# Encoder layer on one core: dealing branch B's gate and projection products over the units, with keys ahead of queries in the second half

## The chip, the core and the metric

One core of a Trainium2 chip runs the kernel. Its engines work side by side and each follows its own queue in order: PE (TensorE, matrix products), DVE (VectorE), ACT (ScalarE), POOL (GpSimd) and SP (SyncE, which issues most DMAs). The metric is the device time of one execution in microseconds (us). Three executions took 2141.36, 2141.90 and 2141.91, median 2141.9. A separate execution was recorded by the profiler.

## The reference

A bidirectional encoder layer on a prompt of 1024 tokens and a sample of 512, width 1024, inputs in float32:

```python
z = xn @ w_in                    # q_A k_A v_A q_B k_B v_B gate_A gate_B
o_a = grouped-query attention with axial rotary embedding (8 heads of 64)
o_b = neighbourhood attention on a grid 64 wide: windows of 8 rows x 16 columns,
      plus a learned bias per head and offset (8 heads of 64)
merged = sigmoid(ga) * (o_a @ w_proj_a) + sigmoid(gb) * (o_b @ w_proj_b)
x = x + merged @ w_out
x = x + relu(rmsnorm(x) @ w_mlp_up) ** 2 @ w_mlp_down
y = rmsnorm(x)
```

The change concerns `o_b` of the prompt, the projections `q_B` and `k_B`, and the product of `gate_B`, which runs between them.

## The kernel before

The sample goes through branches A and B and the merge first, then the prompt, then both together through the MLP (from about 1200 us). Operands are kept as a high and a low part in a 32-bit format that PE takes at full rate, and a product is three matmuls (high by high, high by low, low by high): `mm3`, L216. One such triple of 128 x 128 by 128 x 512 is called a *step*. Making the two parts is `split`: ACT copies the high part (L199), DVE subtracts for the low part in two halves (L206).

**Branch B of the prompt** runs in 32 *units* (h, j): head h of 8, and a strip j of the grid in the order 1, 2, 0, 3. I number them: unit u = 4h + place of j, so unit 14 is (3, 0). Its tiles carry h and j: `sbs_3_0` are its scores. In each pass i of the main loop, in this order:

- `s_unit`: PE makes unit i's scores in `sbs` (four matmuls, PSUM pool of two). POOL makes the masks `bms`, DVE adds them (`sbss`, L1039), ACT takes the exponential (`pbs`, L1065), DVE a reciprocal, POOL scales.
- `turn`, one unit later: DVE transposes blocks (L1077), POOL writes them to DRAM (`tbs`, L1079).
- `fetch_t`, two units later: SP reads them back turned (`bhs`, L1088), behind what stands on SP by then; `prep_v` loads the values `vss` of the next head.
- `t_unit`, three units later: ACT and DVE make the high and low part of `bhs` (L1099, L1100).
- `v_unit`, four units later, at the end of that pass: PE makes the outputs `obs` from six matmuls; ACT and DVE add their halves (`ot_Bs`, `os_Bs`), SP stores.
- Between them PE is filled by *gate steps* (`fill.pull(f)`: `gpss`, 8 weight chunks of 16 steps each for the two halves of 512 tokens; a chunk's `raw_gs` is loaded and `w_gs` split while the chunk before is worked on) and by *projection steps* of the next pair of heads (`qkproj`: `pqbs` queries, `pkbs` keys, 8 steps for each half of the tokens). The projection of a pair of heads is done in the seventh and eighth unit of the pair before. Its outputs are taken from PSUM by ACT and DVE: queries L978 and L980, keys L999 and L1001, one DMA (L1005).

The projection's weights are loaded by `load_qk` and split by entries of `held`, one at a time at fixed passes.

PE runs this stretch in the order in which the code stands. The other engines' orders are fixed when the program is built, by a scheduler that places each instruction by when its inputs are due; `note` and `behind` put scores, exponentials and fetches behind certain weight splits (L186 to L195). `fill.drain` at pass 25 empties the gate, and projection A (`ppas`, `w_pas`) follows; its output halves `oXs` are split in between.

Of the kernel before, what the change touches and what calls it, by code (L numbers as in the profile page):

```python
# [20 lines left out]
NC8 = D // P  # L21
# [40 lines left out]
def encoder(ctx: ExitStack, tc: tile.TileContext, xs, outs, w):  # L62
# [30 lines left out]
    def mm(name):  # L93
        return pmm.tile([P, 512], F32, tag="mm", name=name)
# [91 lines left out]
    def note(engine, op):  # L186
        if held_pe:
            firm[engine].append(op.ins)
# [230 lines left out]
    def run(tr, nxt, first):  # L419
        N, x, T, NT, NB = tr.N, tr.x, tr.T, tr.NT, tr.NB  # L420
# [107 lines left out]
        for g in range(2):  # L528
            with phase(f"phR{N}_{g}") as ph:
# [28 lines left out]
                held = [] if first and fresh else None  # L558
# [354 lines left out]
        with phase(f"phB{N}") as ph:  # L913
# [41 lines left out]
            def qkproj(pr, wqk, dest):  # L955
                wq, wk = wqk
                qT = slot([P, 2, T], F32R, f"qB{N}_{pr}")
                kT = [slot([P, 2, T], F32R, f"kB{N}_{pr}_{e}") for e in range(2)]
                dest[pr] = (qT, kT)
                for tb in range(NB):  # L960
                    cs = slice(tb * 512, tb * 512 + 512)
                    pq = mm(f"pqb{N}_{pr}_{tb}")
                    for k in range(NC8):
                        mm3(pq, wq[k][0], wq[k][1], xh(tb, k), xl(tb, k), k == 0, k == NC8 - 1)
                        yield
                    for e in range(2):
                        hs = slice(64 * e, 64 * e + 64)
                        ls = slice(64 - 64 * e, 128 - 64 * e)

                        src = pq[hs].rearrange("p (r j c) -> p j r c", j=4, c=16)  # L970

                        def strip_view(s_):
                            return qT[s_, e, :].rearrange("p (j r c) -> p j r c", j=4, c=16)[
                                :, :, tb * 8 : tb * 8 + 8, :
                            ]

                        dst_h, dst_l = strip_view(hs), strip_view(ls)
                        note("ACT", nc.scalar.activation(dst_h, src, AF.Copy, scale=0.125))  # L978
                        for jj in range(4):
                            op = nc.vector.scalar_tensor_tensor(  # L980
                                dst_l[:, jj],
                                src[:, jj],
                                0.125,
                                dst_h[:, jj].bitcast(F32),
                                op0=ALU.mult,
                                op1=ALU.subtract,
                            )
                            note("DVE", op)
                    pk = mm(f"pkb{N}_{pr}_{tb}")
                    for k in range(NC8):  # L990
                        mm3(pk, wk[k][0], wk[k][1], xh(tb, k), xl(tb, k), k == 0, k == NC8 - 1)
                        yield
                    for e in range(2):
                        hs = slice(64 * e, 64 * e + 64)
                        ls = slice(64 - 64 * e, 128 - 64 * e)

                        both = (hs, ls) if e == 0 else (hs,)
                        for os_ in both:
                            nc.scalar.activation(kT[e][os_, 0, cs], pk[hs], AF.Copy)  # L999
                        for os_ in both:  # L1000
                            nc.vector.tensor_tensor(  # L1001
                                kT[e][os_, 1, cs], pk[hs], kT[e][hs, 0, cs].bitcast(F32), op=ALU.subtract
                            )
                        if e == 1:
                            nc.gpsimd.dma_start(kT[e][ls, :, cs], kT[e][hs, :, cs])  # L1005

            qk = {}
            def s_unit(u, before=None):
                h, j = u
                ct = (0, 1, 1, 2)[j]  # L1010
                c0 = (0, 8, 24, 32)[j]
                jr = (16, 8, 8, 0)[j]
                s = big(f"sb{N}_{h}_{j}")
                for hf in range(halves):
                    r0 = 0 if hf == 0 else 4
                    ir = 4 if hf == 0 else 0
                    if j != 2:
                        bm = ph.tile([P, nkey], F32, tag="bm", name=f"bm{N}_{h}_{j}_{hf}", bufs=4)
                        nc.gpsimd.tensor_tensor(
                            bm.rearrange("p (r c) -> p r c", c=32),  # L1020
                            rects[h][:, ir : ir + kr_n, jr : jr + 32],
                            msk[:, hf * 3 + ct, :].rearrange("p (r c) -> p r c", c=32),
                            op=ALU.add,
                        )
                        bms[hf] = bm
                    q0 = j * (T // 4) + hf * P
                    so = s[:, hf * 512 : hf * 512 + nkey]
                    for i in range(2):
                        kv = qk[h // 2][1][h % 2][:, i, :].rearrange("p (r c) -> p r c", c=GRID_W)[
                            :, r0 : r0 + kr_n, c0 : c0 + 32  # L1030
                        ]
                        mul(so, qk[h // 2][0][:, h % 2, q0 : q0 + P], kv, start=(i == 0), stop=(i == 1))
                sums = []
                for hf in range(halves):
                    nm = f"{N}_{h}_{j}_{hf}"
                    sb = ph.tile([P, nkey], F32, tag="sb", name=f"sbs{nm}", bufs=2)
                    nm_ = sml.tile([P, 1], F32, tag="nm", name=f"nmb{nm}")
                    with behind("DVE"):
                        nc.vector.tensor_tensor_reduce(  # L1039
                            out=sb,  # L1040
                            in0=s[:, hf * 512 : hf * 512 + nkey],
                            in1=bms[hf],
                            op0=ALU.add,
                            op1=ALU.min,
                            scale=-1.0,
                            scalar=3e38,
                            accum_out=nm_,
                        )
                    sums.append((sb, nm_))
                if before is not None:  # L1050
                    before()
                ps = []
                pm = ph.tile([P, halves * nkey], F32, tag="pb", name=f"pb{N}_{h}_{j}", bufs=4 // halves)
                if u in moved:
                    pm = pm.rearrange("p (b f k i) -> p b f k i", b=4, f=halves, i=32)
                for hf, (sb, nm_) in enumerate(sums):
                    nm = f"{N}_{h}_{j}_{hf}"
                    l = sml.tile([P, 1], F32, tag="l", name=f"lb{nm}")
                    p = pm[:, :, hf] if u in moved else pm[:, hf * nkey : (hf + 1) * nkey]
                    to, of = p, sb  # L1060
                    if u in moved:
                        to = p.rearrange("p b k i -> p k b i")
                        of = sb.rearrange("p (k b i) -> p k b i", b=4, i=32)
                    with behind("ACT"):
                        nc.scalar.activation(to, of, AF.Exp, bias=nm_, scale=-1.0, accum_out=l)  # L1065
                    rl = sml.tile([P, 1], F32, tag="rl", name=f"rlb{nm}")
                    nc.vector.reciprocal(rl, l)
                    nc.gpsimd.tensor_scalar(p, p, rl, 1.0, op0=ALU.mult, op1=ALU.mult)
                    ps.append(p)
                PT[u] = pm if u in moved else ps  # L1070
# [103 lines left out]
            for i in range(n + 4 - NB):  # L1174
                if moved:
                    slot_no[0] = i
                if i < n - 8:
                    f = (5 if i < 2 else 2 + i % 2) if NB == 1 else 5 - (i % 6 == 5)
                else:
                    f = 3 + i % 2 if NB == 1 else 8  # L1180
                if NB == 2 and i == n - 11:
                    pa = proj_a(ph, raw_here)
                    next(pa)
                if i < n:
# [10 lines left out]
                    if moved and h > 0:  # L1195
                        with behind("SP"):
                            prep_v(h, j)
                    if i % 8 == 6 and i + 2 < n:

                        qp = qkproj(i // 8 + 1, wqk, qk)  # L1200
                        for _ in range(NC8):
                            next(qp)
                    if i % 8 == 7 and qp is not None:
                        for _ in qp:
# [15 lines left out]
                if NB == 1 and i == n - 8:  # L1220
                    fill.drain()
                    fill.add(pa)
                if held and (i in (4, 5) if i < 8 else i % 8 in (2, 4)):
                    held.pop(0)()
                if i == 3:
                    wqk = load_qk(1, held)
                if oa_held and i >= (n - 9 if NB == 2 else n - 11):
                    oa_held.pop(0)()
                if qp is not None and NB == 2:
                    for _ in range(NC8):  # L1230
                        next(qp)
                fill.pull(f - f // 2)
                for u in due_v.get(i, ()):
# [726 lines left out]
```

## Time and profile before

| | before |
|---|---|
| median of three executions | 2141.9 us |
| profiled execution | 2144.5 us |
| its span (first to last instruction) | 2142.7 us |
| granted clock of TensorE, mean | 0.996 |
| PE busy | 2102.9 us (98%) |
| DVE busy | 1484.2 us (69%) |
| ACT busy | 1141.0 us (53%) |
| POOL busy | 374.0 us (17%) |
| prompt's branch B units on PE | 798.6 to 998.2 us, then projection A |

The profile takes one execution. Its lines give a start, a duration, the engine, the source line and the tile; in square brackets stands the idle time before an instruction and what released it. A granted clock of 0.5 in a stretch means TensorE at half speed there. A wait whose releaser is not known is called "issue".

### The profile page before, as it was taken

The numbers are of one execution on the slowest core, as the hardware profiler recorded it, in microseconds if no ns is written. First come the engines' busy times: TensorE is split into PE (matmuls) and PEld (weight loads), VectorE is DVE, ScalarE is ACT, GpSimd is POOL, SyncE is SP. The second block draws the span as 40 slices with busy tenths as digits, with TensorE's granted clock in tenths as the row PEclk, the third lists the DMA queues.
The fourth block names the chain that finished last, engine by engine and source line by source line (L and its number), as shares of the span: only waits on it lengthen the run. The fifth ranks groups of instructions, "written<-read, shape, count | busy, mean of one in ns | idle before, by whom it ended". The sixth has DMA issues, their size and how long they took to land.

```text
span 2142.7 us, 32014 instructions
## 1 busy us (share of the span) xinstructions
PE 2102.9 (98%) x10871; PEld 1841.3 (86%) x10871; DVE 1484.2 (69%) x2793; ACT 1141.0 (53%) x2487; POOL 374.0 (17%) x470
## 2 busy tenths in 40 slices
PE   9999999999999999989999999999999999999998
PEld 8888778988897888877888899999999988888886
DVE  6665786767657756766882877778777777659662
ACT  6664653767656645544531566566655633334442
POOL 2232310323233215533200200003000000000000
PEclk9999999999999999999999999999999999999999
DMA  6437557520122136666572666578544799688561
GB/s 190 133 97 212 156 159 252 184 73 25 54 80 70 42 95 190 206 206 184 176 247 101 209 193 192 164 252 208 159 145 158 260 353 341 213 274 279 165 206 59
DMA packets 337002, 372.95 MB, mean 174 GB/s; under 512 B 33471, under 2 KB 269639, under 8 KB 336839
## 3 DMA queue, kind: packets, MB, share of 16 engines
q1 hardware_dynamic: 296695, 296.17, 44.6%
q10 hardware_dynamic: 31072, 45.11, 6.0%
q0 software_dynamic: 9072, 29.63, 4.7%
q8 instruction: 86, 1.41, 0.3%
q14 instruction: 77, 0.63, 0.1%
HBM read 274.29 MB, written 97.32 MB: 173 GB/s over the span
## 4 chain that ended last, share of the span: by engine, by line
PE 52%; DVE 1%; issue 0%; DMA 0%; ACT 0%; SPq 0%; POOLq 0%; POOL 0%; ACTq 0%; DVEq 0%
PE dn L212 20%; PE ua L212 6%; PE ud L212 6%; PE uc L212 6%; PE ops L212 4%; PE ub L212 3%; PE ppbs L212 2%; PE ppas L212 2%; PE dnf L212 2%; PE pt L353 0%; PE obs L212 0%; PE gpss L212 0%; PE sbs L212 0%; PE ptbs L1109 0%; DVE A L1435 0%
## 5 line engine op out<-in xcount | busy, mean ns | idle before, releaser
L212 PE MATMUL dn<-wd,ah 128*128 128x512 f32 x1248 | 384.3, 389 | 0.0
L212 PEld LDWEIGHTS dn<-wd,ah 128*128 128x128 f32 x1248 | 234.3, 188 | 48.6
L212 PE MATMUL dn<-wd,al 128*128 128x512 f32 x624 | 242.8, 389 | 0.0
L1434 ACT ACTIVATE ah<-ar 128x512 fp32r<-128x512 f32 x168 | 103.9, 627 | 197.5 <-PE dn L212 186.1
L212 PE MATMUL gpss<-xs_0h,w_gs 128*128 128x512 f32 x512 | 189.7, 404 | 0.8 <-DVE ot_Bs L471 0.4
L1435 DVE TENSOR_TENSOR al<-ar,ah 128x512 fp32r<-128x512 f32 x168 | 113.8, 686 | 74.1 <-ACT ah L1434 66.9
L212 PE MATMUL ud<-B,A 128*128 128x384 f32 x768 | 143.6, 334 | 0.7 <-DVE c L1552 0.7
L212 PE MATMUL uc<-B,A 128*128 128x384 f32 x768 | 143.7, 334 | 0.0
L212 PE MATMUL ua<-B,A 128*128 128x384 f32 x768 | 138.8, 334 | 0.0
L212 PEld LDWEIGHTS dn<-wd,al 128*128 128x128 f32 x624 | 117.2, 188 | 24.2
L780 POOL TENSOR_SCALAR ps<-ps,rls 128x1024 f32<-128x1024 f32 (+1 forms) x96 | 96.9, 1010 | 225.7 <-DVE rls L779 200.4
L212 PEld LDWEIGHTS ud<-B,A 128*128 128x128 f32 x768 | 134.0, 188 | 1.1 <-DVE c L1552 1.1
L212 PEld LDWEIGHTS uc<-B,A 128*128 128x128 f32 x768 | 134.1, 188 | 0.2 <-ACT A L1434 0.2
L212 PEld LDWEIGHTS ua<-B,A 128*128 128x128 f32 x768 | 133.7, 188 | 0.2
L820 DVE TENSOR_TENSOR ptls<-pTs,pths 128x512 fp32r<-128x512 f32 x160 | 107.6, 686 | 37.7 <-ACT pths L819 36.9
L819 ACT ACTIVATE pths<-pTs 128x512 fp32r<-128x512 f32 x160 | 94.1, 598 | 73.9 <-PE pTs L814 71.6
L212 PE MATMUL ops<-wh_os,mgs 128*128 128x512 f32 x384 | 119.5, 390 | 0.0
L774 DVE TENSOR_REDUCE nms<-ss 128x1 f32<-128x1024 f32 (+1 forms) x96 | 99.8, 1040 | 25.6 <-PE ss L772 25.0
L212 PEld LDWEIGHTS gpss<-xs_0h,w_gs 128*128 128x128 f32 x512 | 97.1, 190 | 19.1 <-DVE w_gs L206 0.7
L180 POOL TENSOR_TENSOR rs_f<-ms_f,mhalf 128x1 f32<-128x1 f32 x6 | 4.0, 666 | 590.7 <-DVE ms_f L176 590.7
L777 ACT ACTIVATE ps<-ss,nms 128x1024 f32<-128x1024 f32 (+1 forms) x96 | 93.3, 972 | 22.7 <-DVE nms L774 20.1
L814 PEld LDWEIGHTS pTs<-ident,ps 128*128 128x128 f32 x640 | 77.9, 140 | 28.5 <-POOL ps L780 4.5
(288 smaller groups left out, 5158.5 us busy)
## 6 DMA issues: line engine op xcount, KB each, us to landing
ar<-ud SPq DMA_DIRECT2D x120, 512.0 KB, 5.1
br<-in_w_mlp_down_dram SPq DMA_DIRECT2D x72, 512.0 KB, 5.4
rawu<-in_w_mlp_up_dram SPq DMA_DIRECT2D x64, 512.0 KB, 4.2
ud<-c ACTq DMA_DIRECT2D x128, 192.0 KB, 2.8
raw_gs<-in_w_in_dram SPq DMA_DIRECT2D x32, 512.0 KB, 4.0
ud<-cs SPq DMA_DIRECT2D x64, 192.0 KB
tbs<-pbs POOLq DMA_DIRECT2D x24, 384.0 KB, 3.4
bhs<-tbs SPq DMA_DIRECT2D x96, 96.0 KB, 2.2
```

The lines of the kernel that those rows point to most:

```text
L180: nc.gpsimd.tensor_tensor(r[:, :n], m[:, :n], mhalf[:, :n], op=ALU.pow)
L212: op = nc.tensor.matmul(out, a, b, **kw)
L774: nc.vector.tensor_reduce(nm_, s, axis=AX.X, op=ALU.max, negate=True)
L777: nc.scalar.activation(p, s, AF.Exp, bias=nm_, accum_out=l)
L780: nc.gpsimd.tensor_scalar(p, p, rl, 1.0, op0=ALU.mult, op1=ALU.mult)
L814: nc.tensor.transpose(pt[:, j * P : (j + 1) * P], PP[u, j][:, kc * P : (kc + 1) * P], ident)
L819: nc.scalar.activation(hi, pt, AF.Copy)
L820: nc.vector.tensor_tensor(lo, pt, hi.bitcast(F32), op=ALU.subtract)
L1434: nc.scalar.activation(hi, src, AF.Copy)
L1435: nc.vector.tensor_tensor(lo, src, hi.bitcast(F32), op=ALU.subtract)
```

## The change

It touches branch B of the prompt (`NB == 2`); the sample's keeps its numbers. There are four parts.

1. `qkproj` projects queries of the first half, keys of the first half, **keys of the second half, then queries of the second half** (before: queries, keys, queries, keys).
2. The gate steps per unit are 8, 7, 7, 6, 6, 0, 0, 4 over eight units (before: 5, and 4 in every sixth).
3. The projection starts in the sixth unit of eight: 4 + 4 steps there, 6 + 6 in the seventh, the other 12 in the eighth (before: 8 + 8 in the seventh and 16 in the eighth).
4. `load_qk(1)` and the two splits of its weights come one pass earlier.

```diff
-                for tb in range(NB):
+                def queries(tb):
                     cs = slice(tb * 512, tb * 512 + 512)
                     pq = mm(f"pqb{N}_{pr}_{tb}")
...
+                def keys(tb):
+                    cs = slice(tb * 512, tb * 512 + 512)
                     pk = mm(f"pkb{N}_{pr}_{tb}")
...
+                yield from queries(0)
+                yield from keys(0)
+                if NB == 2:
+                    yield from keys(1)
+                    yield from queries(1)
...
-                if i < n - 8:
-                    f = (5 if i < 2 else 2 + i % 2) if NB == 1 else 5 - (i % 6 == 5)
+                if NB == 1:
+                    f = (5 if i < 2 else 2 + i % 2) if i < n - 8 else 3 + i % 2
                 else:
-                    f = 3 + i % 2 if NB == 1 else 8
+                    f = (8, 7, 7, 6, 6, 0, 0, 4)[i % 8] if i < n - 8 else 8
...
-                    if i % 8 == 6 and i + 2 < n:
+                    if i % 8 == (6 if NB == 1 else 5) and i < n - 2 - 8 * (NB - 1):
 
                         qp = qkproj(i // 8 + 1, wqk, qk)
-                        for _ in range(NC8):
+                    if qp is not None and i % 8 < 7:
+                        for _ in range(NC8 if NB == 1 else 2 * (i % 8) - 6):
                             next(qp)
...
-                if held and (i in (4, 5) if i < 8 else i % 8 in (2, 4)):
+                if held and (i % 8 in (2, 4) if i > 7 else i in ((4, 5), (3, 4))[NB - 1]):
                     held.pop(0)()
-                if i == 3:
+                if i == 4 - NB:
                     wqk = load_qk(1, held)
...
                 if qp is not None and NB == 2:
-                    for _ in range(NC8):
+                    for _ in range(2 * (i % 8) - 6):
                         next(qp)
```

Three places of the built programs show what it does to the engines' orders; the numbers at the end of names tell buffers apart.

On **PE** at the end of unit 13 and the start of unit 14. Before, unit 14's scores were followed by the first query steps:

```order
L212 MATMUL obs_2_2_10443<-bhs_2_2_10272,vss_2_10059 128x2x128 x6
L212 MATMUL sbs_3_0_10457<-kBs_1_1_9773,qBs_1_9771 128x384 x4
L212 MATMUL pqbs_2_0_10498<-xs_0h_4501,w_bqs_2_9986 128x512
L212 MATMUL pqbs_2_0_10498<-xs_0l_4503,w_bqs_2_9986 128x512
L212 MATMUL pqbs_2_0_10498<-xs_0h_4501,w_bqs_2_9986 128x512 x2
```

Now the queries of the first half stand in unit 13, and the keys follow the scores:

```order
L212 MATMUL obs_2_2_10487<-bhs_2_2_10291,vss_2_10056 128x2x128 x6
L212 MATMUL sbs_3_0_10501<-kBs_1_1_9742,qBs_1_9740 128x384 x4
L212 MATMUL pkbs_2_0_10549<-xs_0h_4501,w_bks_2_9989 128x512
L212 MATMUL pkbs_2_0_10549<-xs_0l_4503,w_bks_2_9989 128x512
L212 MATMUL pkbs_2_0_10549<-xs_0h_4501,w_bks_2_9989 128x512 x2
```

The first product behind these scores now needs the keys' weight `w_bks_2`, and no query step stands in front of it.

On **DVE**, where the outputs of unit 13 (`ot_Bs_3_2`) are added up. Before, the low part for unit 14's outputs (`bhs_3_0`, L1100) came after the split of gate weight 6, unit 17's scores (`sbss_4_2`) and a transpose:

```order
L471 TENSOR_TENSOR ot_Bs_3_2_10879<-obs_3_2_10872,ot_Bs_3_2_10879 64x512
L206 TENSOR_TENSOR w_gs_3328_6_10727<-raw_gs_3328_6_0_10725,w_gs_3328_6_10727 128x512 x2
L1039 ISA sbss_4_2_0_10826,nmbs_4_2_0_10827<-sbs_4_2_10821,bms_4_1_0_10747 128x384
L1039 ISA nmbs_4_2_0_10827 128x1
L1039 ISA sbss_4_2_1_10829,nmbs_4_2_1_10830<-sbs_4_2_10821,bms_4_1_1_10751 128x384
L1039 ISA nmbs_4_2_1_10830 128x1
L1077 STREAM_TRANSPOSE pbs_4_1_10764<-pbs_4_1_10764 128x768
L1067 RECIPROCAL rlbs_4_2_0_10838<-lbs_4_2_0_10836 128x1
L1067 RECIPROCAL rlbs_4_2_1_10843<-lbs_4_2_1_10841 128x1
L1100 TENSOR_TENSOR bhs_3_0_10775<-bhs_3_0_10775 128x768
```

Now it stands ahead of them:

```order
L471 TENSOR_TENSOR ot_Bs_3_2_10890<-obs_3_2_10883,ot_Bs_3_2_10890 64x512
L1110 TENSOR_TENSOR bhs_3_0_10763<-bhs_3_0_10763 128x768
L483 TENSOR_TENSOR os_Bs_3_2_10893<-ot_Bs_3_2_10890 64x256
L206 TENSOR_TENSOR w_gs_3328_6_10782<-raw_gs_3328_6_0_10780,w_gs_3328_6_10782 128x512 x2
L1049 ISA sbss_4_2_0_10828,nmbs_4_2_0_10829<-sbs_4_2_10823,bms_4_1_0_10735 128x384
L1049 ISA nmbs_4_2_0_10829 128x1
L1049 ISA sbss_4_2_1_10831,nmbs_4_2_1_10832<-sbs_4_2_10823,bms_4_1_1_10739 128x384
L1049 ISA nmbs_4_2_1_10832 128x1
L1087 STREAM_TRANSPOSE pbs_4_1_10752<-pbs_4_1_10752 128x768
```

`bhs_3_0` moved up past one split, two score rows and a transpose; the split of gate weight 6, which unit 18 now uses from its third gate step on, moved behind it and behind `os_Bs_3_2`.

On **SP**, the load of gate weight 7. Before, it stood behind the fetches of units 16 and 17 (`bhs_4_1`, `bhs_4_2`), and that weight was first used in unit 22:

```order
L1088 DMA bhs_4_1_10914<-tbs_4_1_10833 32x4x192 x4
L942 DMA vss_4_10782<-vds_4660 32x4x128 x4
L1238 DMA zgs_1_4662<-sgs_3328_5_0_10861 128x512
L1238 DMA obds_4664<-os_Bs_3_2_10882 64x256
L1088 DMA bhs_4_2_10986<-tbs_4_2_10901 32x4x192 x4
L942 DMA vss_4_10782<-vds_4660 32x4x128 x4
L245 DMA raw_gs_3328_7_0_11000<-in_w_in_dram 128x8x128
```

Now it follows unit 16's fetch and four loads of values:

```order
L1249 DMA zgs_1_4662<-sgs_3328_4_1_10778 128x512
L1249 DMA obds_4664<-os_Bs_3_1_10820 64x256
L1098 DMA bhs_4_1_10926<-tbs_4_1_10835 32x4x192 x4
L942 DMA vss_4_10770<-vds_4660 32x4x128 x4
L245 DMA raw_gs_3328_7_0_10943<-in_w_in_dram 128x8x128
L1249 DMA zgs_1_4662<-sgs_3328_5_0_10860 128x512
```

The load moved up by one fetch, one load of values and two stores; the weight's first use moved from unit 22 to the last gate step of unit 20, and on DVE its split stands directly ahead of unit 19's score rows.

## The prediction

> **What bounds the kernel now.** I read the page first, then PE's waits in the prompt's branch B (its units run from 798 to 998 us), then the busy shares by stretch, then the stalls one at a time.
>
> ```profile
> span 2142.7 us, 32014 instructions
> PE 2102.9 (98%) x10871; PEld 1841.3 (86%) x10871; DVE 1484.2 (69%) x2793; ACT 1141.0 (53%) x2487; POOL 374.0 (17%) x470
> ```
>
> TensorE (PE) is busy 98% of the span, so only its idle time and a slow clock can be won. The change leaves the number of its products alone. From here everything is PE's lost time in branch B. Its waits between 770 and 1070 us (engine, tile, what ended the wait: total, times, longest):
>
> ```profile
> PE obs L212 <- issue: 6.8, 2, 4.7
> PE sbs L212 <- DVE kBs L1001: 2.3, 2, 1.8
> PE ppas L212 <- DVE w_pas L206: 1.5, 1, 1.5
> ...
> PE pqbs L212 <- DVE ot_Bs L471: 0.7, 1, 0.7
> ...
> PE obs L212 <- DVE bhs L1100: 0.2, 1, 0.2
> ```
>
> The `ppas` wait is behind the units, and this change leaves its surroundings alone. The other rows add up to 6.8 + 2.3 + 0.7 + 0.2 = 10.0 us. The busy shares by stretch (start:end, length, PE busy, then the granted clock after POOL) show where they lie:
>
> ```profile
> 798.00:857.00 59.00, 58.35 (x274) 48.92 (x273) 41.85 (x99) 30.17 (x61) 29.28 (x37) 1.00 0.61 185
> 857.00:918.00 61.00, 60.31 (x295) 51.42 (x294) 43.90 (x108) 32.20 (x65) 30.54 (x38) 1.00 0.69 207
> 918.00:987.60 69.60, 62.77 (x292) 53.09 (x291) 45.80 (x112) 34.61 (x67) 24.39 (x34) 0.95 0.69 203
> ...
> 942.30:949.20 6.90, 5.89 (x18) 5.25 (x19) 3.26 (x6) 1.84 (x4) 0.74 (x2) 0.51 0.80 226
> 990.00:993.60 3.60, 3.60 (x10) 3.00 (x10) 3.51 (x9) 2.58 (x6) 1.11 (x2) 0.53 0.57 174
> ```
>
> The first 16 units lose 1.3 us together. The third round of eight, from 918 us, loses 6.8 us and runs partly at half clock. The two short stretches are those at half speed: from the end of the 4.68 us stall below, 943.31, to 949.2 is 5.9 us, at half speed 2.9 us of work lost; 3.4 us from 990 lose 1.7 us. So the units lose **10.0 + 4.6 = 14.6 us**, and that is all the change can win. The three long stalls:
>
> ```profile
> 933.52 0.72 PE L212 MATMUL obs<-bhs,vss 128*128 128x256 f32 x4 [2.14 <-issue]
> 943.31 1.62 PE L212 MATMUL obs<-bhs,vss 128*128 128x256 f32 x6 [4.68 <-issue]
> 989.81 1.11 PE L212 MATMUL sbs<-kBs,qBs 128*128 128x384 f32 x3 [1.82 <-DVE kBs L1001]
> ```
>
> "issue" names no releaser, so I looked at what makes `bhs` for these two products, on DVE and ACT:
>
> ```profile
> 928.86 1.29 DVE L206 TENSOR_TENSOR w_gs<-raw_gs,w_gs 128x512 fp32r<-128x512 f32 x2 [0.27 <-ACT w_gs L199]
> 930.07 0.55 DVE L1039 CUSTOM_DVE_ANT_0 sbss<-sbs,bms 128x384 f32<-128x384 f32 x1
> ...
> 932.23 1.09 DVE L1100 TENSOR_TENSOR bhs<-bhs 128x768 fp32r<-128x768 f32 x1
> ...
> 942.25 0.96 DVE L1100 TENSOR_TENSOR bhs<-bhs 128x768 fp32r<-128x768 f32 x1 [0.57 <-ACT bhs L1099]
> 940.77 0.61 ACT L1065 ACTIVATE pbs<-sbss,nmbs 128x384 f32<-128x384 f32 x1 [2.85 <-DMA tbs<-pbs]
> 941.39 0.83 ACT L1099 ACTIVATE bhs<-bhs 128x768 fp32r<-128x768 f32 x1
> ```
>
> Unit 14's low part (932.23) is queued on DVE behind the gate weight's split and unit 17's scores; it ends where PE resumes. Unit 15's high part (941.39) stands on ACT behind an exponential of unit 19, which waits 2.85 us for the buffer that unit 17's transposed block leaves. Both are queue positions, not missing data.
>
> **The change part by part.** PE's own times: a gate or projection step is three products.
>
> ```profile
> 870.64 0.39 PE L212 MATMUL gpss<-xs_1h,w_gs 128*128 128x512 f32 x1
> 870.87 0.89 PE L212 MATMUL obs<-bhs,vss 128*128 128x256 f32 x6
> 871.60 0.88 PE L212 MATMUL sbs<-kBs,qBs 128*128 128x384 f32 x4
> 872.31 0.40 PE L212 MATMUL gpss<-xs_1h,w_gs 128*128 128x512 f32 x1
> ```
>
> By the starts, a product takes 0.23 us, so a step 0.69; a unit's `obs` 0.73 and its scores 0.71. Eight units hold 70 steps before (38 gate, 32 projection) and 70 after: no work is removed, only dealt differently.
>
> *What goes.* In the new order unit 14's low part stands on DVE ahead of the gate weight and of unit 17's scores, and unit 15's high part on ACT ahead of the exponentials of units 18 and 19. Their blocks are fetched a unit earlier than they are used. I take 2.14 + 4.68 + the 2.9 of half clock as gone: **-9.7**. The 0.69 (unit 15's projection, which opens an accumulator and waits until `obs` output has left one) goes, since unit 15 now goes on with one already open, and the 0.16 before an early `obs` goes too, since the unit that it ends is longer: **-0.85**. The first unit's 0.49 and unit 24's 1.82 with its 1.7 change their cause and are priced again below. Nothing of the 14.6 is then left but what follows.
>
> *Keys first.* Units 6, 14 and 22 now begin with keys. Their weight's split is queued behind the previous unit's `obs` output:
>
> ```profile
> 885.55 0.87 PE L212 MATMUL sbs<-kBs,qBs 128*128 128x384 f32 x4
> 885.75 0.59 ACT L470 ACTIVATE ot_Bs<-obs 64x512 f32<-64x512 f32 x1 [3.52 <-PE obs L212]
> 886.25 1.04 ACT L199 ACTIVATE w_bks<-raw_bks 128x1024 fp32r<-128x1024 f32 x1
> 887.32 1.29 DVE L206 TENSOR_TENSOR w_bks<-raw_bks,w_bks 128x512 fp32r<-128x512 f32 x2 [0.27 <-ACT w_bks L199]
> ```
>
> `obs` ended as the next scores began, at 885.55. The high part is done 1.74 us later, the first low half 2.4. Before, eight query steps hid that; now the scores alone do, 0.71 us. PE waits 1.0 for the high part and, as the low part is first used by a step's third product, 0.3 more: 1.3 each in units 14 and 22 (unit 6's weight is split in units 3 and 4): **+2.6**. Were the split's inputs early and the queue free, 0; without any overlap 1.7 each.
>
> *Gate weight 6.* It is first used in unit 18's third gate step, 0.71 + 2 x 0.69 = 2.1 us after unit 13's `obs` at the end of unit 17, low half 2.55 after. DVE now does that `obs`'s output (about 1.4 us after it ended), unit 14's low part (0.96), the sum's second half (0.4) and then the first half of the split (0.65): 3.4. **+0.9**, from 0 to 1.3.
>
> *Gate weight 7.* Its load is now directly behind unit 16's fetch on SP, and that waits for unit 16's transposed block:
>
> ```profile
> 930.71 1.79 POOL L1019 TENSOR_TENSOR bms<-rects,msks 128x384 f32<-128x384 f32 x2 [6.93 <-DVE nmbs L1039]
> 932.44 0.62 POOL L1079 DMA_DIRECT2D tbs<-pbs  x1
> ...
> DMA to landing us min/median/max: 1.9/3.3/6.2
> ...
> 936.06 1.89 SPq L1088 DMA_DIRECT2D bhs<-tbs  x4
> 938.01 2.26 SPq L942 DMA_DIRECT2D vss<-vds  x4
> ...
> raw_gs<-in_w_in_dram SPq DMA_DIRECT2D x32, 512.0 KB, 4.0
> ```
>
> Counted from unit 16's start: units 16 and 17 hold 8 and 7 steps, so unit 17 ends at 6.9 + 6.3 = 13.2. DVE then needs 2.8 to the gate split, 1.2 for it, 0.95 for unit 17's two score rows: 18.1. POOL's pair of masks (1.8) and the block's DMA (3.3) land at 23.2; four fetches (1.95) and four loads of values (2) put the weight's load at 27.1, landed at 31.1, high part at 32.1. PE reaches it in the last gate step of unit 20: units 18 (with its 0.9) and 19 end at 26.0, scores and five steps at 30.1. The gap is 2.1 plus 0.3 for the low half: **+2.4**. Unit 19's score rows stand on DVE behind that split, so unit 21's scores find their PSUM buffer late: **+0.6**. A landing of 1.9 instead of 3.3 leaves about 1.6 of the 3.0, one of 6.2 makes it 5.9. The profile of before has no such wait.
>
> *Queries last.* The scores now wait for eight low pieces instead of key pieces:
>
> ```profile
> 780.45 0.59 ACT L978 ACTIVATE qBs<-pqbs 64x512 fp32r<-64x512 f32 x1 [4.75 <-PE pqbs L212]
> 782.61 0.92 DVE L980 SCALAR_TENSOR_TENSOR qBs<-pqbs,qBs 64x128 fp32r<-64x128 f32 x4 [0.66 <-ACT qBs L978]
> 985.55 0.76 DVE L206 TENSOR_TENSOR w_pas<-raw_pas,w_pas 128x256 fp32r<-128x256 f32 x2 [1.80 <-ACT w_pas L199]
> 988.39 1.36 DVE L1001 TENSOR_TENSOR kBs<-pkbs,kBs 64x512 fp32r<-64x512 f32 x2
> ```
>
> Undisturbed, that is 783.53 - 780.45 = 3.1 us. Cover in front of unit 0's second half is three gate steps and half the scores, 2.4: **+0.7**. For units 8 and 16 the cover is 3.8 (four gate steps, `obs`, half the scores), with one other item in the queue: **+0.3** for both. For unit 24 the last piece stands behind the weight of projection A, two score rows, a transpose and a reciprocal; from 985.55 to 988.39 these took 2.84. So 3.1 + 2.8 - 3.8 = **+2.1**, from 0 (items done early) to 3.
>
> *Clock.* New stalls of 2.1 to 2.4 us may halve the clock behind them. In these rows 1.82 did for 3.4 us (1.7 lost), 4.68 did for 6.8, and the 2.14 did not. I take one of the two: **+1.7**, bounds 0 and 4.6. The Trainium skill, "TensorE: Matmul & The Clock Gate", section "HAM oscillation — how this bites in real kernels", gives idle gaps over about 3.4 us as what throttles; this trace's 1.82 us gap contradicts that and its 2.14 us gap agrees. By that rule this term would be 0 and the sum the third rival's.
>
> **Sum.** 2.6 + 0.9 + 2.4 + 0.6 + 0.7 + 0.3 + 2.1 + 1.7 = 11.3 lost after, against 14.6: 3.3 us shorter. The profiled execution took 2144.5 us (span 2142.7 and 1.8 around it), so 2141.2 for its like; against the median of 2141.9, **2138.6 us**, 0.15% less. A measurement of this kernel tells about 0.2% (4.3 us) from no change.
>
> **Rivals.**
> 1. *The new waits are not there* (chance 0.20). The weights' loads and splits are put in by position in a queue; if the items ahead of them finish sooner than I chained them, weights 6 and 7 arrive in time and no stall reaches the clock. Left are 2.6 + 0.7 + 0.3 + 2.1 = 5.7, 8.9 saved: 2133.0. For it: rounds one and two lose only 1.3 us with the same queues. Against it: the third round has the same chain and lost 6.8.
> 2. *Slower by gate weight 7* (0.20). It lands later than 31.1 because the transposed block takes 6.2 rather than 3.3: stalls 5.9 instead of 3.0, and behind it 2.9 of half clock as after the 4.68, besides 1.7 after unit 24. Lost 2.6 + 0.9 + 5.9 + 0.7 + 0.3 + 2.1 + 4.6 = 17.1, 2.5 slower: 2144.4. With that clock loss it decides where weight 7's two stalls pass 3.4 us; a slow load behind the slow block adds 2 more and passes 0.2%: 2146.5. For it: two slow-clock stretches now. Against: the median landing.
> 3. *No stall is followed by half clock* (0.15): without the 1.7, 5.0 saved, 2136.9. The 2.14 us stall speaks for it, the 1.82 against.
> 4. *The stalls stay* (0.10): units 14 and 15 may wait for their fetched blocks, not for a queue place, and the reordering does not do what it says. Then 4.7 and 2.9 remain, and the new waits partly stand in their shadow: 2141.9.
>
> **How the numbers follow.** My forecast has 0.35. Faster by over 0.2% (below 2137.6): rival 1, two thirds of rival 3, a fifth of the forecast's spread, 0.37. Slower by over 0.2% (above 2146.2): half of rival 2, and some of what I may have missed, 0.12. Within: 0.51. The range takes in rival 1 and all of rival 2 but its extreme: 2131.5 to 2145.5.
>
> **What would show it.** In the changed profile, `obs` should have no "issue" wait near units 18 and 19. `pkbs` should wait 1.3 us for `w_bks`, twice; `gpss` for `w_gs`, twice, 0.9 and 2.4; `sbs` once for its buffer and for `qBs` in units 0 and 24. One clock dip of 3.4 us should be left. If `gpss` never waits for `w_gs`, rival 1 holds; if its wait passes 5 us, rival 2. A new wait behind 1000 us would be a cost that I left out.

## The result, and the profile after

The changed kernel took 2147.2 us (median of 10 runs, 2145.6 to 2149.0) against 2142.7 for the kernel before in the same comparison: ratio 1.0025, 95% interval 1.0016 to 1.0034. It is slower, by about 5 us; 2138.6 (2131.5 to 2145.5), shorter than before, had been forecast. The profiled execution's span grew from 2142.7 to 2146.4 us.

PE's waits of the changed kernel between 770 and 1075 us (engine, tile, what ended the wait: total, times, longest):

```profile
PE obs L212 <- ACT kBs L1002: 6.1, 1, 6.1
PE gpss L212 <- ACT w_gs L199: 1.9, 2, 1.6
PE pkbs L212 <- ACT w_bks L199: 1.8, 2, 0.9
PE obs L212 <- DVE bhs L1110: 1.7, 1, 1.7
PE ppas L212 <- DVE w_pas L206: 1.5, 1, 1.5
PE obs L212 <- DVE ot_Bs L471: 1.0, 1, 1.0
PE obs L212 <- ACT bhs L1109: 0.8, 1, 0.8
...
PE gpss L212 <- DVE w_gs L206: 0.2, 1, 0.2
```

Without `ppas` these are 13.5 us, against 10.0 before. The old 2.1 and 4.7 us waits for `bhs` are gone, as forecast; one wait of 6.1 us, which no part of the forecast names, costs nearly as much as both. The busy shares by stretch show where it lies, and what the clock lost (the granted clock stands after POOL):

```profile
798.00:860.00 62.00, 62.00 (x293) 52.73 (x292) 42.76 (x110) 31.80 (x66) 29.06 (x40) 1.00 0.66 189
860.00:920.00 60.00, 58.28 (x284) 49.14 (x283) 42.27 (x105) 31.60 (x65) 25.55 (x36) 1.00 0.65 190
920.00:990.00 70.00, 59.87 (x263) 48.77 (x262) 43.53 (x94) 30.57 (x57) 23.91 (x33) 0.93 0.68 201
951.00:955.00 4.00, 4.00 (x14) 3.40 (x14) 3.99 (x14) 2.64 (x6) 3.47 (x5) 0.60 0.43 160
974.00:982.00 8.00, 5.46 (x18) 4.93 (x19) 4.93 (x12) 5.03 (x9) 1.80 (x3) 0.57 0.33 90
```

The first round has no stall left (62.00 of 62.00). The third loses 10.1 us, and again runs twice at half clock: 4.0 x 0.4 = 1.6 us lost from 951, and about half of the 5.4 us of work from 976.5 to 982, 2.6 us. Stalls and clock cost 13.5 + 4.2 = 17.7 us, 3.1 more than the 14.6 before; that is most of the span's 3.7.

**The 6.1 us.** On PE the stalled product is unit 18's `obs`, in unit 22. Its chain, read back from PE through DVE, ACT, POOL and SP:

```profile
976.54 1.62 PE L212 MATMUL obs<-bhs,vss 128*128 128x256 f32 x6 [6.13 <-ACT kBs L1002]
975.52 0.92 DVE L980 SCALAR_TENSOR_TENSOR qBs<-pqbs,qBs 64x128 fp32r<-64x128 f32 x4 [0.93 <-ACT qBs L978]
974.89 0.59 ACT L978 ACTIVATE qBs<-pqbs 64x512 fp32r<-64x512 f32 x1
973.09 0.61 ACT L1075 ACTIVATE pbs<-sbss,nmbs 128x384 f32<-128x384 f32 x1 [8.28 <-DMA tbs<-pbs]
965.24 0.58 POOL L1089 DMA_DIRECT2D tbs<-pbs  x1
963.80 0.98 DVE L1087 STREAM_TRANSPOSE pbs<-pbs 128x768 f32<-128x768 f32 x1
961.64 1.29 DVE L206 TENSOR_TENSOR w_bks<-raw_bks,w_bks 128x512 fp32r<-128x512 f32 x2 [0.26 <-ACT w_bks L199]
961.43 0.59 SPq L245 DMA_DIRECT2D raw_pas<-in_w_proj_a_dram  x1
962.89 0.80 SPq L848 DMA_DIRECT2D rawos<-oads  x2
```

`obs` starts 0.1 us after DVE has taken the last query piece out of its accumulator (975.52 + 0.92 = 976.44). The view names a copy of the keys on ACT (L1002) as the releaser; the last of these had ended by 976.1, 0.4 us before `obs` starts. Four accumulators exist (`pmm`, four buffers), and all four are taken: gate chunk 7, which one step had opened at the end of unit 20 and no step continued in units 21 and 22; the queries of unit 21; and both halves of the keys, now made one after the other. So `obs` must wait for the queries to be drained. The second query drain stands on ACT behind unit 22's exponential, and that waited 8.28 us for a buffer of transposed scores: unit 20's block went out at 965.24 and landed at 973.1. As I read the chain, it went out late, since its transpose stood on DVE behind the split of the keys' weight; and it took 7.8 us, since projection A's first loads had been issued 2.3 to 3.8 us before. The runs below test this.

In the kernel before, the same exponential waited too, and PE did not:

```profile
967.43 0.62 ACT L1065 ACTIVATE pbs<-sbss,nmbs 128x384 f32<-128x384 f32 x1 [3.65 <-DMA tbs<-pbs]
971.83 0.89 PE L212 MATMUL obs<-bhs,vss 128*128 128x256 f32 x6
```

At its `obs` three accumulators were taken, and one was free.

### The profile page after: what moved, and what is told of

It is laid out like the page before. It is cut to its first block, busy times and chain, and to the rows that moved or that the text cites. A ratio compares the mean times of both kernels' runs of the same rounds, so it can differ in the third digit from the quotient of the medians.

```text
span 2146.4 us, 32017 instructions
## 1 busy us (share of the span) xinstructions
PE 2103.1 (98%) x10871; PEld 1840.2 (86%) x10871; DVE 1486.6 (69%) x2793; ACT 1141.2 (53%) x2487; POOL 369.9 (17%) x470
## 4 chain that ended last, share of the span: by engine, by line
PE 65%; DVE 1%; DMA 1%; issue 1%; ACT 1%; POOL 0%; SPq 0%; ACTq 0%; POOLq 0%; DVEq 0%
PE dn L212 20%; PE ua L212 6%; PE ud L212 6%; PE uc L212 6%; PE gpss L212 5%; PE ops L212 4%; PE ub L212 3%; PE ppbs L212 2%; PE pqbs L212 2%; PE ppas L212 2%; PE dnf L212 2%; PE pTs L814 1%; PE pkbs L212 1%; PE obs L212 1%; PE sbs L212 1%
```

## The experiments

All ratios are against the kernel before, in the same comparison. The medians come from five comparisons, in which the kernel before took 2141.4 to 2142.7 us, so runs are compared by their ratios.

| run | what it is | us, median | ratio (95%) |
|---|---|---|---|
| | the change | 2147.2 | 1.0025 (1.0016 to 1.0034) |
| e1 | change, projection's order undone | 2146.8 | 1.0024 (1.0014 to 1.0034) |
| e3 | change, gate chunk 7 not opened early | 2143.5 | 1.0009 (1.0000 to 1.0019) |
| e5 | change, keys' weight split a pass earlier | 2141.2 | 1.0000 (0.9991 to 1.0009) |
| e6 | change, projection A's loads a pass later | 2144.6 | 1.0016 (1.0007 to 1.0026) |
| e2 | before, with the projection's new order alone | 2138.5 | 0.9985 (0.9976 to 0.9994) |
| e7 | e3 and e5 | 2140.0 | 0.9990 (0.9981 to 1.0000) |
| e9 | e3, e5 and e6 | 2141.8 | 1.0001 (0.9992 to 1.0011) |
| e10 | e7, gate weight split later | 2141.1 | 0.9995 (0.9985 to 1.0004) |
| e11 | e2, gate weight split later | 2139.9 | 0.9988 (0.9979 to 0.9997) |
| e12 | e2, three gate steps dealt earlier | 2141.1 | 0.9993 (0.9984 to 1.0002) |
| e13 | e2, fetched block ahead of exponentials | 2137.2 | 0.9977 (0.9967 to 0.9986) |
| e14 | e13, gate weight split later | 2137.2 | 0.9977 (0.9967 to 0.9986) |

### Which part makes the 6.1 us: e1, e3, e5, e6

e1 undoes the order:

```diff
-                    yield from keys(1)
-                    yield from queries(1)
+                    yield from queries(1)
+                    yield from keys(1)
```

> The changed kernel with the projection's order put back (queries, keys, queries, keys); steps and splits as changed. Theory A (accumulators): in unit 22 the outputs of unit 18 find all four PSUM accumulators taken (gate chunk 7 opened by one step, three of the projection), whatever the order of the projection; the 6.1 us wait of obs stays at 5 to 7 us and the time stays near 2147 (1.0 to 1.003 of the kernel before). Rival B (keys first is to blame): the wait goes and the time falls by 6 us or more, to about 2140. Both: the two 0.9 us waits for the keys' weight stay, since keys still begin unit 14 and 22.

```profile
973.70 1.62 PE L212 MATMUL obs<-bhs,vss 128*128 128x256 f32 x6 [6.10 <-ACT kBs L1002]
```

The wait stayed at 6.1 us and the time at the change's. The order of keys and queries is not to blame; a third half of the projection in flight at that `obs`, of whichever kind, is enough. Of the two waits for the keys' weight only unit 22's stayed (0.9 us), since in unit 14 that split came earlier in the orders of ACT and DVE.

e3 takes one step from unit 20 to unit 23:

```diff
-                    f = (8, 7, 7, 6, 6, 0, 0, 4)[i % 8] if i < n - 8 else 8
+                    f = (8, 7, 7, 6, 6 - i // 20, 0, 0, 4 + i // 20)[i % 8] if i < n - 8 else 8
```

> The changed kernel with 5 instead of 6 gate steps in unit 20 and 5 instead of 4 in unit 23, so that gate chunk 7 is not opened before the projection. Theory A (accumulators): one of four is free in unit 22, the 6.1 us wait of obs falls under 1 us, the 1.6 us wait for gate weight 7 goes as well, and the clock dip behind it; 6 to 10 us less than the changed kernel, 2137 to 2141. Rival B (obs waits for its own data, late through the exponential of unit 22): the wait stays above 4 us, and the time falls by no more than 3 us.

Its longer waits from unit 21 on, with unit 22's `obs` and the drain of the queries:

```profile
952.37 0.99 PE L212 MATMUL sbs<-kBs,qBs 128*128 128x384 f32 x4 [3.21 <-DVE nmbs L1049]
961.18 0.50 PE L212 MATMUL pkbs<-xs_0h,w_bks 128*128 128x512 f32 x1 [0.92 <-ACT w_bks L199]
969.77 0.89 PE L212 MATMUL obs<-bhs,vss 128*128 128x256 f32 x6
974.62 0.92 DVE L980 SCALAR_TENSOR_TENSOR qBs<-pqbs,qBs 64x128 fp32r<-64x128 f32 x4
975.68 0.47 PE L212 MATMUL pqbs<-xs_1h,w_bqs 128*128 128x512 f32 x1 [1.54 <-DVE qBs L980]
995.67 1.62 PE L212 MATMUL obs<-bhs,vss 128*128 128x256 f32 x6 [2.50 <-issue]
```

`obs` in unit 22 (969.77) does not wait at all, although unit 22's exponential still started as late as 972.4: the 6.1 us were a missing accumulator. The next taker of one, the second half of the queries, then waits 1.5 us for the same drain. The time fell by less than was expected (2143.5 against 2137 to 2141). The `obs` of unit 25 waits 2.5 us where it had waited 1.7, with half clock behind it (1.4 us lost). And the wait for gate weight 7 did not go but moved: unit 21's scores (`sbs`) wait 3.2 us for unit 19's score rows, which stand on DVE behind that weight's split:

```profile
950.06 1.29 DVE L206 TENSOR_TENSOR w_gs<-raw_gs,w_gs 128x512 fp32r<-128x512 f32 x2 [3.38 <-ACT w_gs L199]
951.27 0.55 DVE L1049 CUSTOM_DVE_ANT_0 sbss<-sbs,bms 128x384 f32<-128x384 f32 x1
```

e5 pops the keys' weight a pass earlier in the second and third round:

```diff
-                if held and (i % 8 in (2, 4) if i > 7 else ...):
+                if held and (i % 8 in (2, 4 - (NB == 2)) if i > 7 else ...):
```

> The changed kernel with the split of the keys' weight one pass earlier in the second and third round. All theories: the two 0.9 us waits of pkbs go. Theory C (the split in front of the transpose of unit 20 makes unit 22's exponential late): tbs goes out 2 to 4 us earlier, lands before projection A's loads crowd the DMA engines, and the 6.1 us wait falls to under 3; time 2140 to 2144. If it does not matter for that wait: 1 to 2 us less, 2145 to 2146.

Both waits of `pkbs` went. In unit 22:

```profile
959.27 0.58 POOL L1089 DMA_DIRECT2D tbs<-pbs  x1
963.40 0.62 ACT L1075 ACTIVATE pbs<-sbss,nmbs 128x384 f32<-128x384 f32 x1 [2.06 <-DMA tbs<-pbs]
968.75 0.92 DVE L980 SCALAR_TENSOR_TENSOR qBs<-pqbs,qBs 64x128 fp32r<-64x128 f32 x4
969.76 1.62 PE L212 MATMUL obs<-bhs,vss 128*128 128x256 f32 x6 [2.83 <-issue]
```

The exponential starts 963.4 instead of 973.1, `obs` waits 2.8 us, and again starts 0.1 us after the last query piece. This one edit gives back all that the change cost. Unit 20's block goes out at 959.27, ahead of projection A's first loads (960.04), and lands in 4.1 us; so this run mends the late transpose and the slow landing together.

e6 puts the line `if NB == 2 and i == n - 11` for projection A's first loads to `n - 10`:

> The changed kernel with projection A's first loads (three, 1.25 MB) one pass later. Theory D (they crowd the DMA engines, share 0.9, so that unit 20's transposed block lands 7.8 us after its issue instead of 3.4): it lands in 3 to 5 us, unit 22's exponential starts 3 to 4 us earlier, the 6.1 us wait falls to 2 to 3 us; time 2142 to 2144, unless projection A then waits. Rival: the landing stays above 6 us, time 2147.

```profile
963.84 0.58 POOL L1089 DMA_DIRECT2D tbs<-pbs  x1
967.06 0.62 ACT L1075 ACTIVATE pbs<-sbss,nmbs 128x384 f32<-128x384 f32 x1 [3.64 <-DMA tbs<-pbs]
969.50 0.92 DVE L980 SCALAR_TENSOR_TENSOR qBs<-pqbs,qBs 64x128 fp32r<-64x128 f32 x4 [0.93 <-ACT qBs L978]
970.52 0.95 PE L212 MATMUL obs<-bhs,vss 128*128 128x256 f32 x6 [1.52 <-ACT kBs L1002]
995.27 1.16 PE L212 MATMUL obs<-bhs,vss 128*128 128x256 f32 x6 [3.79 <-DVE bhs L1110]
```

Issued at 963.84, the block landed at 967.06: 3.2 us instead of 7.8. The stall fell to 1.5 us; the time, 2144.6, is a little above what was expected. The `obs` of unit 25 now waits 3.8 us where it had waited 1.7: its high part stands on ACT behind an exponential whose buffer came free only at 991.57, 5.6 us after unit 22's block went out (985.98), right behind a load for projection A (985.62). The loads were part of the cause of the 6.1 us; that they also make the new wait is argued, not tested.

So three runs bear out the chain: the missing accumulator (e3), the slow landing alone (e6), the late transpose together with the landing (e5).

### The order alone, and the mends together: e2, e7, e9, e10

e2 puts `qkproj` of the change into the kernel before, and nothing else.

> The kernel before with nothing but the new order of the projection (queries, keys, keys, queries). If the order is harmless, as the run with it undone suggests: the two obs waits of 2.1 and 4.7 us stay, no wait of 6 us appears in unit 22 (two gate steps and eight projection steps stand between there, and only three accumulators are taken at its obs), the wait of unit 24's scores changes from keys to queries and stays 1 to 3 us; ratio 0.999 to 1.001. If the order costs by itself, above 1.002.

```profile
PE obs L212 <- issue: 6.6, 2, 4.5
...
PE pkbs L212 <- DVE ot_Bs L471: 0.7, 1, 0.7
...
PE obs L212 <- DVE bhs L1110: 0.2, 1, 0.2
```

The two `obs` waits stayed. The wait of unit 24's scores did not change its cause, as I had expected, but vanished: no `sbs` row is left that counts, and with it went the first unit's 0.5 us and the half clock behind 990 us. The order alone is **faster** (0.9985, expected 0.999 to 1.001); the other three parts without it (e1) are slower (1.0024). These three were not run one by one.

e7 joins e3 and e5, e9 adds e6:

> The changed kernel with both mends: gate chunk 7 not opened in unit 20, and the keys' weight split a pass earlier. If the two causes add: no wait of obs above 1 us in unit 22, no pkbs wait; the 3.2 us wait of unit 21's scores behind gate weight 7's split stays; ratio 0.998 to 0.999. If they are two ways to mend one thing: same time as the better of the two alone, ratio 1.000.

> As the one with both mends, and projection A's first loads a pass later. If the landing of unit 20's block still matters once an accumulator is free: 1 to 2 us less than that kernel. If not (it is off the path then): the same within 1 us, or slower where projection A's weights come late behind 1000 us.

In e7 nothing waits in unit 22 and `pkbs` does not wait, so the two add: together they take 0.35% off the change, alone 0.16% and 0.25%. 3.4 us of unit 21's scores are left, the largest stall. e9 took the second of its outcomes: its `obs` near 993 us waits 3.3 us where that of e7 waits 1.7, and the later loads gain nothing.

e10 takes that stall away by a later split:

```diff
-                        if k == 2:
+                        if k == (6 if NB == 2 and goff == 3328 else 2):
```

> As the one with both mends, and the branch B gate's weight is split after 7 instead of 3 steps of the chunk before. Theory E (a split put into the ACT and DVE queues before its load has landed blocks unit 19's score rows behind it): the 3.2 us wait of unit 21's scores goes, and with it the 0.5 us in unit 18; 3 to 4 us less than the kernel with both mends, ratio 0.996 to 0.998. Rival (scores are late through other work): the wait stays above 2 us.

The 3.4 us of unit 21's scores went, so the cause was right; the price was not, and the 0.5 us in unit 18 stayed. `obs` waited 2.3 us at 903 (it had waited 0.3) and 3.7 us at 969, as I see it since with every instruction that the scheduler moves other queue places change. The time did not fall; this run does not say more.

### A version that beats both: e11 to e14

The waits of units 14 and 15 are what is left in e2. e11 is e2 with the later split of e10. e12 deals differently:

```diff
-f = ... else 5 - (i % 6 == 5)
+f = ... else 5 - (i % 6 == 5) + (i in (16, 17, 18)) - (i in (20, 21, 22))
```

> The kernel before with the new order of the projection, and the branch B gate's weight split after 7 instead of 3 steps of the chunk before; steps are dealt as before. Theory E (a weight's split put early into the DVE queue holds up score rows and transposes behind it): unit 17's score rows and unit 16's transpose now stand ahead of gate weight 6's split, unit 17's block goes out earlier, and the two obs waits of 2.1 and 4.5 us shrink to under 3 together, without the 3 us of half clock; 4 to 7 us less than the order alone, ratio 0.995 to 0.997. Rival (blocks are late for other reasons): both stay, ratio 0.998 to 0.999.

> The kernel before with the new order, and one gate step moved from each of units 20, 21, 22 to units 16, 17, 18 (6 and 4 instead of 5 and 5). The obs waits of units 18 and 19 depend on when the block of units 14 and 15 is ready, and three more steps stand ahead of them by unit 19: if dealing more steps ahead of a wait is what covers it, they shrink by 1 to 2 us and the ratio is 0.997 to 0.998; if queue positions set it, they stay or grow, ratio 0.998 to 1.000.

In e11 unit 14's wait fell from 2.1 to 0.25 us, but unit 15's stayed at 4.5 and a 1.8 us wait appeared near 994 us; the time did not fall below that of e2. In e12 unit 14's wait fell to 1.4, but unit 15's grew to 5.0: more steps ahead did not cover it. That left its place on ACT, behind unit 19's exponentials. e13 puts it ahead, for which the block's high part is noted so that later exponentials stand behind it:

```diff
-                    nc.scalar.activation(hi, lo.bitcast(F32), AF.Copy)
+                    note("ACT", nc.scalar.activation(hi, lo.bitcast(F32), AF.Copy))
```

> The kernel before with the new order of the projection, and the high part of a fetched block put ahead of the next unit's exponentials on ACT; in the order it moves only for unit 15 (ahead of unit 19's exponentials). If the 4.5 us wait of unit 15's outputs is a queue place (its block was fetched long before), it falls to 2 to 3 us, what is left being the low part behind a transpose on DVE, the half clock behind it stays or halves; ratio 0.996 to 0.9975. If the block itself is late, the wait stays at 4 to 5 us and the ratio at 0.9985.

> The same, and the gate's weight split after 7 steps instead of 3. The waits of unit 14 (2.1 us with the early split) and of unit 15 both shrink, to under 2.5 together; ratio 0.995 to 0.997, unless the split put later makes waits of its own near 990 us (1.7 us in the run with the split later alone): then 0.997 to 0.998.

```profile
936.11 0.84 ACT L1109 ACTIVATE bhs<-bhs 128x768 fp32r<-128x768 f32 x1
939.70 0.61 ACT L1075 ACTIVATE pbs<-sbss,nmbs 128x384 f32<-128x384 f32 x1 [2.75 <-DMA tbs<-pbs]
940.90 0.96 PE L212 MATMUL obs<-bhs,vss 128*128 128x256 f32 x6 [3.19 <-issue]
```

In e13 the high part runs at 936.1 instead of behind the exponential that waits until 939.7. The stall fell from 4.5 to 3.2 us (2 to 3 were expected) and half of the half-clock loss went (3.0 to 1.7 us). What is left is the low part, which stands on DVE behind a transpose and starts at 939.18. In e14 the waits of units 14 and 15 are 2.7 us together (under 2.5 expected), and a 1.8 us wait near 991 us, with half clock behind it, takes up the gain. e13 and e14 have the lowest times here, 0.23% under the kernel before and 0.48% under the change (0.9977 against 1.0025); their intervals overlap with that of e2.

## Why the prediction was wrong

**What goes: right.** The 2.14 and 4.68 us and the dip behind them are gone. They are gone in e1 too, which has parts 2 to 4 of the change, and stay in e2, which has part 1 alone: the new dealing removed them, not the order of keys and queries. That the second was a queue place e13 shows from the other side: moving one instruction cut it from 4.5 to 3.2 us.

**The step that failed: the forecast's sum counts engines and queues, and not accumulators.** That all four are taken at unit 22's `obs` stands in no term and in no rival; "nothing of the 14.6 is then left but what follows" put this wait at nothing. I had read that unit 20 opens gate chunk 7 with one step, and used it only to price its weight. I had even seen a wait for an accumulator (0.69 us, unit 15's projection) and let it go, since one is already open there; I did not ask what is open at the next `obs`, where the earlier start of the projection leaves three halves instead of two. 6.1 us of stall and 2.6 of half clock behind it are 8.7 us, about the whole difference between 2138.6 and the 2147.2 measured. That they match is partly luck: the other terms together were 5.8 us too high, and other waits of 3.5 us were not foreseen.

**Where other terms stood.**
- Keys first, 2.6: measured 1.8 (two of 0.92). I had let the low part wait as well; the high part alone set it.
- Gate weight 6, 0.9: measured 0.5 (0.27 and 0.24). Gate weight 7 on PE, 2.4: measured 1.6. The 0.6 for unit 21's scores did not appear on PE in the changed kernel: the gate steps waited for the same weight first. In e3, where this step was gone, it was 3.2. The mechanism was right, and what shows depends on who comes first.
- Queries last, 0.7 + 0.3 + 2.1: measured nothing. I made the scores wait for all eight low pieces. The pieces are of two heads, the first four of the even one, and a pair's first four units use only these. In the changed kernel the eighth piece ended at 994.7 and unit 24's scores started at 991.95:

```profile
989.33 0.88 DVE L980 SCALAR_TENSOR_TENSOR qBs<-pqbs,qBs 64x128 fp32r<-64x128 f32 x4 [0.95 <-ACT qBs L978]
991.95 0.89 PE L212 MATMUL sbs<-kBs,qBs 128*128 128x384 f32 x4
994.38 0.29 DVE L980 SCALAR_TENSOR_TENSOR qBs<-pqbs,qBs 64x128 fp32r<-64x128 f32 x1
```

  This error hid the change's good part: e2, the order alone, is 0.15% faster.
- Clock, 1.7: measured 4.2, since the 6.1 us stall has a dip of its own.
- Not foreseen besides: `obs` waits of 0.8, 1.0 and 1.7 us. The 1.0 us one, in unit 19, ends when DVE has emptied unit 14's outputs from their accumulator (`ot_Bs`), which fits the same shortage; no run tested it.

**The rivals.** Rivals 1, 3 and 4 did not hold: `gpss` waited for `w_gs`, two stretches ran at half clock, and the waits of units 14 and 15 went. The slower case was given, for gate weight 7 landing late. The time passed even its extreme of 2146.5, by another mechanism. Its link, a transposed block that lands late, was real, at unit 20's block (7.8 us) instead of unit 16's.

**What stays open.** Stalls and clock explain 3.1 of the profiled execution's 3.7 us, and that execution grew by less than the medians (4.5). What the remainder is was not found. One execution is also thin evidence for the clock, which differs between executions of one kernel: of 30 executions of the kernel before, in the comparison of e1, the 11 with a mean granted clock of 0.996 took 2142.4 to 2144.2 us and the 10 with 0.998 took 2139.7 to 2141.4. The profiled execution before, 2144.5 us at 0.996, is one of the longer ones.

## What to carry to other kernels

Before a product is moved, count the accumulators that are open at each product which needs a new one, those of half-finished sums that merely rest there included. An accumulator is free only when its last reader has run, and that reader may stand in a queue behind something that waits for a DMA. And when an output is taken out in pieces, ask which piece the next consumer reads before it is made to wait for the last.

## What was not expected of the hardware

Stalls of about the same length were or were not followed by half clock: the 1.6 us one before 949 us was, the 1.7 us one at 1001 us was not, and in e2 and e13 that of 2.1 us was not. The 3.2 us one of e3, before 952 us, was not either. The Trainium skill, "TensorE: Matmul & The Clock Gate", section "What's actually happening", says that the activity window of 3.4 us runs freely, so that a transition depends on where in the window work falls. That fits the scatter of these rows. Its figure of one idle window does not: half clock came behind 1.6 us of idleness here.

The transposed block of 384 KB landed 7.8 us after its issue while three loads of together 1.25 MB went ahead, and 3.2 us after it when they were put behind it (e6).
